# A diffusion-backbone layer on one core: how the feed-forward blocks mark their PSUM banks, begin and end

## The chip, the cores and the metric

The kernel runs on one core of a Trainium2 chip. The metric is the device time of one execution in microseconds (us): the median of repeated runs. Beside it stands one profiled execution, with its own time and its span (first to last instruction). TensorE (PE in the rows) multiplies into PSUM banks, ScalarE (ACT) and VectorE (DVE) work elementwise, GpSimd (POOL) does small work and issues some transfers, SyncE (SP) issues the others.

## The reference

One layer over 512 latent tokens of 1024 channels, with a context prefix of 256 tokens. What matters here is its end: a SwiGLU feed-forward part with 2816 hidden channels, a gated residual, and a last RMSNorm.

```python
def _swiglu(h, w_in, w_out):
    g, u = jnp.split(h @ w_in, 2, axis=-1)
    return (jax.nn.silu(g) * u) @ w_out

        x = x + g1 * mix_lat
        x = x + g2 * _swiglu(_modulate(x, norm_ffn[l], sh2, sc2), w_ffn_in[l], w_ffn_out[l])
    return _rmsnorm(x, norm_final)          # x / sqrt(mean(x^2) + eps) * norm_final
```

All data is 32-bit. The kernel gets the precision by splitting each operand into a high part (a cast to fp32r) and a low part (what the cast lost), and by adding three products: high by high, high by low, low by high.

## The kernel before, in words

Activations lie transposed: 128 channels on the partitions, tokens along the free axis, so x is 8 tiles of 128x512 (`x1[0..7]`). A "half" is 256 of the 512 tokens. `mm3` issues the three products of each pair of 128x128 weight and moving tile, so a sum over n tiles is 3n matmuls (lines 181 to 183). Weights come by SyncE into `wr` or `ur` tiles; ScalarE makes the high part (`wh`, `gh` or `oh`), VectorE the low part (`wl`, `gl` or `ol`).

The hidden channels are 22 tiles. Tiles 0 to 2 are computed plainly, each as two `Half` objects (one for each half of the tokens), which sum a gate and an up product in two banks. Tiles 3 to 21 go through `strassen`, in three runs (3 to 7, 8 to 14, 15 to 21), each followed by the products of its tiles with the second weight (`ffn_out`). The scheme replaces eight half-size products of a tile by seven: with weight quarters A11, A12, A21, A22 and their sums S1 to S4 it issues, 12 matmuls each, A11, S1, S2 and A12 (`front`) and S3, S4 and A22 (`back`, one tile later). The sums are made by `prepare`: VectorE adds, ScalarE casts the high part, VectorE subtracts for the low part; for A12 and A22 ScalarE writes the negated high part and a GpSimd transfer adds the weight to it.

After the A11 product ScalarE copies the bank `x` to a bank `z` (line 1009), and the S2 product is then added on top of `x`, the A12 product on top of the copied `z`. So S2 cannot start before that copy has read `x`. The S1 product is copied to a tile too (line 1013). For a product to be added to what ScalarE or VectorE put in a bank, a matmul must have written those columns before: four plain matmuls do that for the four `pat` banks (line 1180), ahead of the first run of `strassen`. The first run gets tile 3 prepared beforehand (`p3`); the loop then prepares tile j+1 ahead of the products of tile j, and the order written is the order on ScalarE and VectorE as far as a scheduler, which also moves independent instructions, keeps it.

The end: the last seven hidden tiles (15 to 21) multiply the second weight, for each output tile j and half 21 matmuls (`ffn_out`, line 1170 adds the sum to `x1[j]`). Each finished half tile is squared on ScalarE (`SumSq.add`) and summed on VectorE; for the second half the eighth square stays apart and is summed by TensorE with the rest (`urgent`). `rstd_cols` sums over the partitions by matmuls against ones (line 220), GpSimd raises to the power -1/2 (line 224), `rstd_rows` spreads the row over the partitions by two matmuls (line 232). `final` then multiplies each 128x256 piece by `norm_final` and the row, and SyncE writes two pieces at a time (line 1200).

Of the kernel before, what the change touches and what calls it, by code (L numbers as in the profile page):

```python
# [48 lines left out]
def layer_kernel(ctx: ExitStack, tc, xT, cT, w0, w1, wv0, wv, wada_a, wada_b, par, crow, bg, wpool,  # L49
# [140 lines left out]
    class SumSq:  # L190
# [21 lines left out]
        def rstd_cols(self, c):  # L212

            n = (c.stop - c.start) // P
            bank = self.banks.pop(0) if self.banks else PS("pat" if self.free else "ps")
            for i in range(n):
                o = slice(c.start + i * P, c.start + (i + 1) * P)
                terms = [self.q] + [q for s, q in self.last.items() if s == c.start]
                for t, q in enumerate(terms):
                    nc.tensor.matmul(bank[:, 2 * i:2 * i + 2], q[:, o], ones[:, 0:2], start=t == 0, stop=t == len(terms) - 1)  # L220
            sd = tl("rc", [P, 4], F32, 2)
            V.tensor_scalar(sd[:, :n], bank[:, :2 * n].rearrange("p (i w) -> p i w", w=2)[:, :, 0], 1.0 / D, EPS,
                            ALU.mult, ALU.add)
            nc.gpsimd.tensor_tensor(sd[:, :n], sd[:, :n], mhalf[:, :n], ALU.pow)
            return sd
# [812 lines left out]
    def strassen(lo, hi, p=None):  # L1038

        prev = None  # L1040
        p = p or prepared(lo)
        for j in range(lo, hi + 1):
            f = front(j, p) if j < hi else None
            if j + 1 < hi:
                p = prepared(j + 1)
            b = back(j - 1, *prev) if prev else iter(())
            if f:
                next(f)
                next(f)
# [29 lines left out]
    class Half:  # L1079


        def __init__(self, j, c):
            self.c, (self.wg, self.wu, self.dst) = c, pw[j]
            self.accg, self.accu, self.s = PS(), PS(), S("tmp")

        def gate(self):
            mm3(self.accg[:, self.c], self.wg, hpart(self.c))

        def up(self):
            mm3(self.accu[:, self.c], self.wu, hpart(self.c))  # L1090

        def silu(self):
            nc.scalar.activation(self.s[:, self.c], self.accg[:, self.c], AF.Silu)

        def mul(self):
            V.tensor_mul(self.s[:, self.c], self.s[:, self.c], self.accu[:, self.c])
# [68 lines left out]
    def ffn_out(j, c, w, c0, c1):  # L1165

        turn_[0] += 1
        acc = banks[turn_[0] % 3]
        mm3(acc[:, c], w, half(act[c0:c1], c))
# [9 lines left out]
    for i in range(4, 8):  # L1179
        nc.tensor.matmul(banks[i], B11[0][:, :P], B11[0][:, :T], start=True, stop=True)  # L1180
# [10 lines left out]
    def final(i, sd):  # L1191

        c = HALF[i]
        r = st2.rstd_rows(sd, c)
        for j in range(0, KT, 2):
            if j % 4 == 0:
                raw = tl("wr", [P, WMAX], F32, 3)[:, :2 * T].rearrange("p (j t) -> p j t", j=4)
            for e in range(2):
                V.scalar_tensor_tensor(raw[:, j % 4 + e, :], x1[j + e][:, c], pcol(C_NFIN, j + e), r, ALU.mult, ALU.mult)
            nc.sync.dma_start(out.rearrange("p (j t) -> p j t", j=KT)[:, j:j + 2, c], raw[:, j % 4:j % 4 + 2, :])  # L1200

    wl_ = [wchunk(j, c0, c1, (None, None, "wide", "wide", ("oh", "ol"), ("oh", "ol"), None, None)[j], 16) for j in range(KT)]
    for j in range(4):
        ffn_out(j, HALF[0], wl_[j], c0, c1)
# [6 lines left out]
    final(0, sd)  # L1211
    for j in (6, 7):
        ffn_out(j, HALF[1], wl_[j], c0, c1)
    final(1, st2.rstd_cols(HALF[1]))
# [89 lines left out]
```

## Time and profile before

| | before |
|---|---|
| median of 3 runs | 908.22 us (907.78 to 908.56) |
| the profiled execution's own time | 905.2 us |
| its span | 903.4 us |
| mean granted TensorE clock | 0.990 |
| TensorE busy | 879.0 us, 97% |
| VectorE busy | 613.9 us, 68% |
| ScalarE busy | 428.3 us, 47% |

How to read it: the times in the rows run from the span's start. Matmuls overlap, so a row's own duration (0.28 us for 128x256) is longer than the distance to the next start; an idle time stands in brackets at the instruction that ended it, with the engine, tile and line that released it.

### The profile page before, as it was taken

Reading aid. Unit: us, or ns where it says so; the run is one execution under the profiler, and the core shown is the slowest. Engines: PE = TensorE matmul, PEld = TensorE weight load, DVE = VectorE, ACT = ScalarE, POOL = GpSimd, SP = SyncE. Lnnn points to the kernel's source line nnn. Section 1 sums busy time; section 2 is a strip of 40 time slices with the busy share of each in tenths; the row PEclk is TensorE's granted clock in tenths of the full one; section 3 lists DMA queues with packets and bytes.
Section 4 is the critical chain, followed back from the end, with each engine's and each line's share of the span. In section 5 each row is a group of like instructions: output and inputs, shape, how many; then the busy total and the mean of one; then the engine's idle time right before and its main releaser. Section 6 shows DMA issues by size and latency. Waiting matters only on the chain.

```text
span 903.4 us, 14978 instructions
## 1 busy us (share of the span) xinstructions
PE 879.0 (97%) x5883; PEld 796.5 (88%) x5883; DVE 613.9 (68%) x1194; ACT 428.3 (47%) x806; POOL 63.3 (7%) x92
## 2 busy tenths in 40 slices
PE   7999999999999999999999899999999999999996
PEld 6679888899888998889988699999789998899995
DVE  3679656856688676886778768885366754867644
ACT  3455363555343553435553347674145741666520
POOL 0000010010000100001000000111011100111000
PEclk8999999999999999999999999999999999999998
DMA  9834021322066212662147750375356643766402
GB/s 339 323 118 137 22 85 29 133 74 82 24 214 241 83 58 82 210 234 73 57 152 262 247 189 25 100 192 129 94 153 142 158 122 88 203 141 140 118 1 94
DMA packets 42485, 121.20 MB, mean 134 GB/s; under 512 B 4624, under 2 KB 9392, under 8 KB 41392
## 3 DMA queue, kind: packets, MB, share of 16 engines
q1 hardware_dynamic: 36944, 110.29, 37.0%
q0 software_dynamic: 5472, 9.96, 6.5%
q8 instruction: 46, 0.75, 0.3%
q14 instruction: 23, 0.19, 0.1%
HBM read 116.55 MB, written 3.69 MB: 133 GB/s over the span
## 4 chain that ended last, share of the span: by engine, by line
PE 70%; DVE 13%; DMA 9%; issue 4%; ACT 4%; POOL 0%; SPq 0%; POOLq 0%; DVEq 0%; ACTq 0%
PE ps L181 14%; PE ps L183 14%; PE ps L182 14%; DMA pb<-in_wada_b 6%; DVE wl L152 3%; PE pat L326 3%; PE ps L539 2%; PE ps L540 2%; PE ps L538 2%; PE pat L744 2%; PE pat L742 2%; PE pat L743 2%; PE pat L182 2%; PE pat L181 2%; PE pat L183 2%
## 5 line engine op out<-in xcount | busy, mean ns | idle before, releaser
L181 PE MATMUL ps<-a,wh 128*128 128x512 f32 (+1 forms) x368 | 138.8, 377 | 0.0
L182 PE MATMUL ps<-a,wh 128*128 128x512 f32 (+1 forms) x368 | 138.5, 376 | 0.0
L183 PE MATMUL ps<-a,wl 128*128 128x512 f32 (+1 forms) x368 | 138.3, 376 | 0.0
L151 ACT CAST wh<-wr 128x1024 fp32r<-128x1024 f32 (+3 forms) x80 | 80.8, 1012 | 120.2 <-PE ps L182 94.3
L152 DVE TENSOR_TENSOR wl<-wr,wh 128x1024 fp32r<-128x1024 f32 (+3 forms) x80 | 94.3, 1180 | 36.6 <-ACT wh L151 35.4
L183 PE MATMUL ps<-act,wl 128*128 128x512 f32 (+1 forms) x224 | 80.1, 359 | 3.0 <-DVE wl L152 3.0
L181 PE MATMUL ps<-act,wh 128*128 128x512 f32 (+1 forms) x224 | 80.3, 359 | 1.6 <-ACT wh L151 1.0
L182 PE MATMUL ps<-act,wh 128*128 128x512 f32 (+1 forms) x224 | 80.1, 358 | 0.3 <-DVE act L171 0.3
L183 PEld LDWEIGHTS ps<-a,wl 128*128 128x128 f32 x368 | 69.3, 188 | 12.6
L181 PEld LDWEIGHTS ps<-a,wh 128*128 128x128 f32 x368 | 69.3, 188 | 12.2
L182 PEld LDWEIGHTS ps<-a,wh 128*128 128x128 f32 x368 | 69.3, 188 | 11.8
L539 PE MATMUL ps<-wl,a 128*128 128x256 f32 (+1 forms) x192 | 54.6, 284 | 2.2 <-DVE wl L152 2.1
L538 PE MATMUL ps<-wh,a 128*128 128x256 f32 (+1 forms) x192 | 54.1, 282 | 0.5 <-DVE tmp L374 0.5
L540 PE MATMUL ps<-wh,a 128*128 128x256 f32 (+1 forms) x192 | 54.1, 282 | 0.0
L183 PEld LDWEIGHTS ps<-act,wl 128*128 128x128 f32 x224 | 42.5, 190 | 10.3 <-DVE wl L152 4.3
L971 POOL DMA_DIRECT2D ol<-in_wffi x38 | 33.5, 889 | 256.3 <-ACT ol L970 119.4
L181 PE MATMUL ps<-hp,gh 128*128 128x256 f32 x176 | 50.3, 286 | 1.0 <-ACT pat L1009 0.9
L1170 DVE SCALAR_TENSOR_TENSOR x<-ps,lb,x 128x512 f32<-128x512 f32 (+1 forms) x32 | 19.7, 617 | 45.4 <-PE ps L183 45.3
L181 PEld LDWEIGHTS ps<-act,wh 128*128 128x128 f32 x224 | 42.4, 190 | 8.0 <-ACT wh L151 1.5
L182 PE MATMUL ps<-hp,gh 128*128 128x256 f32 x176 | 48.8, 277 | 0.0
L183 PE MATMUL ps<-hp,gl 128*128 128x256 f32 x176 | 48.8, 277 | 0.0
L182 PEld LDWEIGHTS ps<-act,wh 128*128 128x128 f32 x224 | 42.6, 190 | 6.7 <-DVE act L171 0.5
(300 smaller groups left out, 2522.4 us busy)
## 6 DMA issues: line engine op xcount, KB each, us to landing
wr<-in_w SPq DMA_DIRECT2D x42, 512.0 KB, 3.6
pb<-in_wada_b SPq DMA_DIRECT2D x32, 512.0 KB, 4.4
wr<-in_wffi SPq DMA_DIRECT2D x25, 512.0 KB, 4.0
ur<-in_wffi SPq DMA_DIRECT2D x19, 512.0 KB, 4.3
ol<-in_wffi POOLq DMA_DIRECT2D x38, 256.0 KB, 5.1
ada<-in_wada_a SPq DMA_DIRECT2D x8, 1024.0 KB, 7.6
wr<-in_wffo SPq DMA_DIRECT2D x16, 448.0 KB, 3.4
x<-in_xT SPq DMA_DIRECT2D x16, 256.0 KB, 5.7
```

What stands on the lines that cost most here:

```text
L151: nc.scalar.copy(wh, raw[:, :n])
L152: V.tensor_sub(wl, raw[:, :n], wh.bitcast(F32))
L181: nc.tensor.matmul(dst, wh, ah, start=first and i == 0, stop=False, skip_group_check=on)
L182: nc.tensor.matmul(dst, wh, al, start=False, stop=False, skip_group_check=on)
L183: nc.tensor.matmul(dst, wl, ah, start=False, stop=last and i == n - 1, skip_group_check=on)
L326: nc.tensor.matmul(acc0[i], w_first[k][i][w], aT[k][x], start=k + w + x == 0, stop=k == KT - 1 and w == 1)
L538: nc.tensor.matmul(acc[:, :n], ah, wh, start=kk == 0, stop=False)
L539: nc.tensor.matmul(acc[:, :n], ah, wl, start=False, stop=False)
L540: nc.tensor.matmul(acc[:, :n], al, wh, start=False, stop=kk == KT - 1)
L742: nc.tensor.matmul(o, sh_, vh[:, s, :], start=n == 0, stop=False)
L971: nc.gpsimd.dma_start(l, dram, accum_op=ALU.add)
L1170: V.scalar_tensor_tensor(x1[j][:, c], acc[:, c], g2[:, j:j + 1], x1[j][:, c], ALU.mult, ALU.add)
```

## The change

Six edits, in the order of the diff. (1) `rstd_cols` issues all matmuls of the first term, then all of the second; only the first of a bank starts it. (2) When `strassen` is given a prepared tile, the first two steps of `front` (A11 with its copy, S1 with its copy) are written ahead of the preparation of the next tile. (3) The plain tile 2 uses the four `pat` banks, from column 0, and the four marking matmuls of line 1180 are gone. (4) `norm_final` is multiplied by ScalarE into tiles (`ur`, `sg`) as soon as a half tile is finished (`gain`). (5) `final` multiplies several pieces by the row in one VectorE instruction and writes them with one transfer: 4 and 4 pieces in the first half, 4, 3 and 1 in the second. (6) In the last block output tiles 0 and 1 first sum six hidden tiles each, and then the seventh each.

```diff
@@ rstd_cols
-            for i in range(n):
-                o = slice(c.start + i * P, c.start + (i + 1) * P)
-                terms = [self.q] + [q for s, q in self.last.items() if s == c.start]
-                for t, q in enumerate(terms):
-                    nc.tensor.matmul(bank[:, 2 * i:2 * i + 2], q[:, o], ones[:, 0:2], start=t == 0, stop=t == len(terms) - 1)
+            terms = [self.q] + [q for s, q in self.last.items() if s == c.start]
+            for t, q in enumerate(terms):
+                for i in range(n):
+                    o = slice(c.start + i * P, c.start + (i + 1) * P)
+                    nc.tensor.matmul(bank[:, 2 * i:2 * i + 2], q[:, o], ones[:, 0:2], start=t + i == 0,
+                                     stop=t == len(terms) - 1, skip_group_check=True)
@@ strassen
+        early = p is not None
         p = p or prepared(lo)
         for j in range(lo, hi + 1):
             f = front(j, p) if j < hi else None
+            if early:
+                next(f)
+                next(f)
             if j + 1 < hi:
                 p = prepared(j + 1)
             b = back(j - 1, *prev) if prev else iter(())
-            if f:
+            if f and not early:
                 next(f)
                 next(f)
+            early = False
@@ Half
-            self.accg, self.accu, self.s = PS(), PS(), S("tmp")
+            tag = "pat" if j == 2 else "ps"
+            self.accg, self.accu, self.s = PS(tag)[:, :TC], PS(tag)[:, :TC], S("tmp")
@@ ffn_out and what follows
+        if acc is None:
+            acc = ffn_bank()
+            mm3(acc[:, c], w, half(act[c0:c1], c))
         V.scalar_tensor_tensor(x1[j][:, c], acc[:, c], g2[:, j:j + 1], x1[j][:, c], ALU.mult, ALU.add)
         if c1 == FT:
-            for c_ in ((c,) if c != ALL else HALF):
-                st2.add(x1[j][:, c_], c_)
+            st2.add(x1[j][:, c], c)
+            if (j, c) != (KT - 1, HALF[1]):
+                gain(j, HALF.index(c))
-    for i in range(4, 8):
-        nc.tensor.matmul(banks[i], B11[0][:, :P], B11[0][:, :T], start=True, stop=True)
+    def gain(j, i):
+        nc.scalar.activation(gained[i][j][:, 0, :], x1[j][:, HALF[i]], AF.Copy, scale=pcol(C_NFIN, j))
@@ final
-        for j in range(0, KT, 2):
-            if j % 4 == 0:
-                raw = tl("wr", [P, WMAX], F32, 3)[:, :2 * T].rearrange("p (j t) -> p j t", j=4)
-            for e in range(2):
-                V.scalar_tensor_tensor(raw[:, j % 4 + e, :], x1[j + e][:, c], pcol(C_NFIN, j + e), r, ALU.mult, ALU.mult)
-            nc.sync.dma_start(out.rearrange("p (j t) -> p j t", j=KT)[:, j:j + 2, c], raw[:, j % 4:j % 4 + 2, :])
+        for lo, hi in zip(cuts, cuts[1:]):
+            g = ur_[lo // 4][:, lo % 4:(hi - 1) % 4 + 1, :] if i == 0 else sg_[:, lo:hi, :]
+            V.tensor_mul(g, g, r.broadcast_to([P, hi - lo, T // 2]))
+            nc.sync.dma_start(out.rearrange("p (j t) -> p j t", j=KT)[:, lo:hi, c], g)
@@ the last block
+    first = [ffn_bank()[:, :T] for _ in range(2)]
+    for part in (slice(0, FT - c0 - 1), slice(FT - c0 - 1, FT - c0)):
+        for j, acc in enumerate(first):
+            mm3(acc[:, HALF[0]], wl_[j][part], half(act[c0:c1], HALF[0])[part], part.start == 0, part.stop == FT - c0)
```

On ScalarE, where the first run of `strassen` begins (tile 3's last copies, then what follows; `pat_6265` is z and `ps_6260` x of tile 3, the `oh`, `ol` and `gh` tiles from number 6277 on belong to tile 4), before:

```order
L970 ACTIVATE ol_6251<-ur_6169 128x512
L966 CAST oh_6277<-wr_6272 128x512
L966 CAST oh_6287<-wr_6272 128x512
L1097 CAST act_6104<-tmp_6193 128x256
L970 ACTIVATE ol_6288<-wr_6272 128x512
L966 CAST oh_6298<-ur_6273 128x512
L970 ACTIVATE ol_6299<-ur_6273 128x512
L170 CAST gh_6283<-sg_6276 128x1024
L1009 COPY pat_6265<-ps_6260 128x256
L170 CAST wh_6294<-sg_6276 128x1024
L1013 COPY tmp_6328<-ps_6263 128x256
```

The same place of the changed kernel (tile 4's numbers begin at 6300):

```order
L971 ACTIVATE ol_6251<-ur_6169 128x512
L1010 COPY pat_6265<-ps_6260 128x256
L1014 COPY tmp_6293<-ps_6263 128x256
L967 CAST oh_6300<-wr_6295 128x512
L1104 CAST act_6104<-tmp_6193 128x256
L967 CAST oh_6310<-wr_6295 128x512
L971 ACTIVATE ol_6311<-wr_6295 128x512
L967 CAST oh_6321<-ur_6296 128x512
L170 CAST gh_6306<-sg_6299 128x1024
L971 ACTIVATE ol_6322<-ur_6296 128x512
L170 CAST wh_6317<-sg_6299 128x1024
L1021 ACTIVATE tmp_6351<-pat_6265 128x256
```

Both copies of tile 3 moved from behind seven copies of tile 4 to ahead of all of them; they still stand behind tile 3's own A22 copy. On TensorE the order of products at this place was A11, S1 of tile 3, A11 of tile 4, S2, A12 of tile 3; it now is A11, S1, S2, A12 of tile 3, A11 of tile 4, then two matmuls of tile 4's S1, six of tile 3's S3, the other ten of S1, the other six of S3, one of S4, and S2 of tile 4. On VectorE the sum of line 1016 (now 1017, it reads the S2 result) stands ahead of tile 4's `gl` instead of behind its `gl` and `wl`.

On TensorE at the start of the last block, where `act_9120` and `act_9121` are the high and low part of the last hidden tile, `ps_6262` and `ps_6260` the sums of output tiles 0 and 1, and `wh_9172`, `wl_9173` the weights of output tile 1, before:

```order
L183 MATMUL ps_6262<-act_9049,wl_9167 128x256
L181 MATMUL ps_6262<-act_9120,wh_9166 128x256
L181 MATMUL ps_6260<-act_8435,wh_9172 128x256
L182 MATMUL ps_6260<-act_8436,wh_9172 128x256
L182 MATMUL ps_6262<-act_9121,wh_9166 128x256
L183 MATMUL ps_6262<-act_9120,wl_9167 128x256
L183 MATMUL ps_6260<-act_8435,wl_9173 128x256
```

And in the changed kernel (the last hidden tile is `act_9116` and `act_9117`, the weights of output tile 1 are `wh_9171` and `wl_9172`; the line of dots stands for the next 14 products into `ps_6260`):

```order
L183 MATMUL ps_6262<-act_9045,wl_9166 128x256
L181 MATMUL ps_6260<-act_8431,wh_9171 128x256
L182 MATMUL ps_6260<-act_8432,wh_9171 128x256
L183 MATMUL ps_6260<-act_8431,wl_9172 128x256
...
L183 MATMUL ps_6260<-act_9045,wl_9172 128x256
L181 MATMUL ps_6262<-act_9116,wh_9165 128x256
L182 MATMUL ps_6262<-act_9117,wh_9165 128x256
L183 MATMUL ps_6262<-act_9116,wl_9166 128x256
L181 MATMUL ps_6260<-act_9116,wh_9171 128x256
```

The first product with the last hidden tile moved from the 19th place of the block to the 37th; the first that reads the low part of tile 1's weights from the 24th to the 21st.

On VectorE at the end of the second half, from the row's first step on, before:

```order
L222 TENSOR_SCALAR rc_9640<-pat_6266 128x2
L1199 SCALAR_TENSOR_TENSOR wr_9645<-x_928_5289,parm,pat_6267 128x256
L1199 SCALAR_TENSOR_TENSOR wr_9645<-x_929_5291,parm,pat_6267 128x256
L1199 SCALAR_TENSOR_TENSOR wr_9645<-x_930_5293,parm,pat_6267 128x256
L1199 SCALAR_TENSOR_TENSOR wr_9645<-x_931_5295,parm,pat_6267 128x256
L1199 SCALAR_TENSOR_TENSOR wr_9652<-x_932_5297,parm,pat_6267 128x256
L1199 SCALAR_TENSOR_TENSOR wr_9652<-x_933_5299,parm,pat_6267 128x256
L1199 SCALAR_TENSOR_TENSOR wr_9652<-x_934_5301,parm,pat_6267 128x256
L1199 SCALAR_TENSOR_TENSOR wr_9652<-x_935_5303,parm,pat_6267 128x256
```

And in the changed kernel:

```order
L1181 SCALAR_TENSOR_TENSOR x_935_5303<-ps_6262,lb,x_935_5303 128x256
L223 TENSOR_SCALAR rc_9644<-pat_6266 128x2
L1215 TENSOR_TENSOR sg_9162<-sg_9162,pat_6267 128x1024
L1215 TENSOR_TENSOR sg_9162<-sg_9162,pat_6267 128x768
L1215 TENSOR_TENSOR sg_9162<-sg_9162,pat_6267 128x256
```

Eight instructions became three; the first transfer of the second half followed the second instruction and now follows the first, which is four pieces wide. On ScalarE a copy of `gain` stands behind each square of the last block.

## Rows read from the trace of the kernel before

**Rows 1.** The page's first part: busy time, share of the span and instruction count of each engine.

```profile
PE 879.0 (97%) x5883; PEld 796.5 (88%) x5883; DVE 613.9 (68%) x1194; ACT 428.3 (47%) x806; POOL 63.3 (7%) x92
```

**Rows 2.** The timeline of TensorE where the first run of `strassen` begins. Columns: start, duration, engine, line, operation, tiles, shape, count; in brackets the idle time before and its releaser.

```profile
581.05 1.09 PE L1180 MATMUL pat<-hp 128*128 128x512 f32 x4
581.98 0.28 PE L181 MATMUL ps<-hp,oh 128*128 128x256 f32 x1
...
585.07 0.39 PE L181 MATMUL ps<-hp,oh 128*128 128x256 f32 x1
...
586.31 0.39 PE L183 MATMUL ps<-hp,ol 128*128 128x256 f32 x1 [0.73 <-DVE ol L968]
...
588.68 0.39 PE L181 MATMUL ps<-hp,gh 128*128 128x256 f32 x1 [0.94 <-ACT pat L1009]
...
594.24 0.28 PE L181 MATMUL ps<-hp,gh 128*128 128x256 f32 x1
```

**Rows 3.** The timeline of ScalarE at the same place.

```profile
583.88 0.63 ACT L970 ACTIVATE ol<-ur 128x512 fp32r<-128x512 f32 x1
584.41 1.12 ACT L966 CAST oh<-wr 128x512 fp32r<-128x512 f32 x2
...
587.33 1.03 ACT L170 CAST gh<-sg 128x1024 fp32r<-128x1024 f32 x1
588.26 0.36 ACT L1009 COPY pat<-ps 128x256 f32<-128x256 f32 x1
```

**Rows 4.** The timeline of VectorE at the same place.

```profile
587.71 0.69 DVE L990 TENSOR_TENSOR sg<-sg,wr 128x512 f32<-128x512 f32 x1
588.39 1.23 DVE L171 TENSOR_TENSOR gl<-sg,gh 128x1024 fp32r<-128x1024 f32 x1
```

**Rows 5.** The timeline of TensorE at the start of the last block.

```profile
850.68 0.28 PE L181 MATMUL ps<-act,wh 128*128 128x256 f32 x1
...
853.48 0.50 PE L181 MATMUL ps<-act,wh 128*128 128x256 f32 x2 [0.52 <-ACT act L170]
...
854.43 0.39 PE L182 MATMUL ps<-act,wh 128*128 128x256 f32 x1 [0.33 <-DVE act L171]
...
857.00 0.28 PE L181 MATMUL ps<-act,gh 128*128 128x256 f32 x1
```

**Rows 6.** The timeline of VectorE at the same place.

```profile
852.36 0.42 DVE L1034 SCALAR_TENSOR_TENSOR tmp<-ps,tmp 128x256 f32<-128x256 f32 x1
852.69 1.08 DVE L152 TENSOR_TENSOR wl<-wr,wh 128x896 fp32r<-128x896 f32 x1
853.69 0.68 DVE L171 TENSOR_TENSOR act<-tmp,act 128x512 fp32r<-128x512 f32 x1
```

**Rows 7.** The timeline of ScalarE there, and one square from the middle of the last block.

```profile
851.41 0.93 ACT L151 CAST wh<-wr 128x896 fp32r<-128x896 f32 x1
852.81 0.62 ACT L170 CAST act<-tmp 128x512 fp32r<-128x512 f32 x1 [0.47 <-DVE tmp L1034]
...
880.13 0.42 ACT L206 ACTIVATE tmp<-x 128x256 f32<-128x256 f32 x1 [2.06 <-DVE x L1170]
```

**Rows 8.** The timeline of TensorE from the first half's row to the end. An fp32 matmul shows as two.

```profile
884.35 0.51 PE L220 MATMUL pat<-ones,tmp 128*128 128x2 f32 x4
...
887.31 0.60 PE L232 MATMUL pat<-ident,rc 128*128 128x128 f32 x4
...
892.58 0.28 PE L183 MATMUL ps<-act,wl 128*128 128x256 f32 x1
...
893.95 0.83 PE L220 MATMUL pat<-ones,tmp 128*128 128x2 f32 x6 [0.63 <-ACT tmp L206]
895.88 0.86 PE L232 MATMUL pat<-ident,rc 128*128 128x128 f32 x4 [1.10 <-POOL rc L224]
```

**Rows 9.** The timeline of VectorE at the end.

```profile
892.90 0.48 DVE L1170 SCALAR_TENSOR_TENSOR x<-ps,lb,x 128x256 f32<-128x256 f32 x1
894.89 0.16 DVE L222 TENSOR_SCALAR rc<-pat 128x2 f32<-128x2 f32 x1 [1.50 <-PE pat L220]
896.77 3.22 DVE L1199 SCALAR_TENSOR_TENSOR wr<-x,parm,pat 128x256 f32<-128x256 f32 x8 [1.73 <-PE pat L232]
```

**Rows 10.** The first issue of an output transfer of the second half on SyncE's queue.

```profile
897.67 0.37 SPq L1200 DMA_DIRECT2D out<-wr  x1
```

**Rows 11.** Stretches of the span. Columns: the stretch, its length, then busy us (and instructions) of PE, PEld, DVE, ACT, POOL, the granted TensorE clock (1.00 is 2.4 GHz, 0.50 is 1.2 GHz), the busy share of the 16 DMA engines, GB/s.

```profile
898.50:899.50 1.00, 0.00 (x0) 0.00 (x0) 1.00 (x3) 0.00 (x0) 0.00 (x0) 0.50 0.91 298
899.50:900.50 1.00, 0.00 (x0) 0.00 (x0) 0.49 (x2) 0.00 (x0) 0.00 (x0) 0.50 1.03 339
900.50:901.50 1.00, 0.00 (x0) 0.00 (x0) 0.00 (x0) 0.00 (x0) 0.00 (x0) 0.50 1.02 336
901.50:902.50 1.00, 0.00 (x0) 0.00 (x0) 0.00 (x0) 0.00 (x0) 0.00 (x0) 0.50 0.23 76
...
12.30:19.00 6.70, 6.70 (x39) 5.21 (x39) 0.16 (x1) 0.95 (x2) 1.01 (x1) 0.50 1.03 429
505.00:510.50 5.50, 2.37 (x10) 1.34 (x9) 4.63 (x6) 2.70 (x3) 0.00 (x0) 1.00 0.40 131
510.70:513.90 3.20, 3.20 (x9) 2.53 (x8) 0.76 (x2) 1.77 (x3) 0.00 (x0) 0.50 0.81 241
585.00:590.00 5.00, 3.25 (x23) 2.85 (x24) 4.98 (x9) 5.00 (x11) 2.63 (x3) 1.00 0.93 250
```

More of the change, by code (lines that the diff above doesn't have):

```diff
@@ L1163, in layer_kernel, with ffn_bank, ffn_out @@
     turn_ = [0]
-    def ffn_out(j, c, w, c0, c1):
+    def ffn_bank():
         turn_[0] += 1
-        acc = banks[turn_[0] % 3]
-        mm3(acc[:, c], w, half(act[c0:c1], c))
+        return banks[turn_[0] % 3]
+    def ffn_out(j, c, w, c0, c1, acc=None):
+        if acc is None:
+            acc = ffn_bank()
+            mm3(acc[:, c], w, half(act[c0:c1], c))
         V.scalar_tensor_tensor(x1[j][:, c], acc[:, c], g2[:, j:j + 1], x1[j][:, c], ALU.mult, ALU.add)
         if c1 == FT:
-            for c_ in ((c,) if c != ALL else HALF):
-                st2.add(x1[j][:, c_], c_)
+            st2.add(x1[j][:, c], c)
+            if (j, c) != (KT - 1, HALF[1]):
+                gain(j, HALF.index(c))
     def wchunk(j, c0, c1, dst=None, skip=0):
         return wload(wffo[j][:, c0 * P:c1 * P], (c1 - c0) * P, dst, skip)[0]
-    for i in range(4, 8):
-        nc.tensor.matmul(banks[i], B11[0][:, :P], B11[0][:, :T], start=True, stop=True)
     for c0, c1 in ((0, 8), (8, 15)):
@@ L1189, in layer_kernel, with final @@
     SumSq.banks = banks[4:]
[L1191 to L1200 removed]
+    ur_ = [tl("ur", [P, D], F32, 2).rearrange("p (j t) -> p j t", j=4) for _ in range(2)]
+    sg_ = tl("sg", [P, 2 * D], F32, 1, LINE).rearrange("p (j t) -> p j t", j=KT)
+    gained = [[ur_[j // 4][:, j % 4:j % 4 + 1, :] for j in range(KT)], [sg_[:, j:j + 1, :] for j in range(KT)]]
+    def gain(j, i):
+        nc.scalar.activation(gained[i][j][:, 0, :], x1[j][:, HALF[i]], AF.Copy, scale=pcol(C_NFIN, j))
+    def final(i, sd, cuts):
+        c = HALF[i]
+        r = st2.rstd_rows(sd, c).rearrange("p (o t) -> p o t", o=1)
+        for lo, hi in zip(cuts, cuts[1:]):
+            g = ur_[lo // 4][:, lo % 4:(hi - 1) % 4 + 1, :] if i == 0 else sg_[:, lo:hi, :]
+            V.tensor_mul(g, g, r.broadcast_to([P, hi - lo, T // 2]))
+            nc.sync.dma_start(out.rearrange("p (j t) -> p j t", j=KT)[:, lo:hi, c], g)
     wl_ = [wchunk(j, c0, c1, (None, None, "wide", "wide", ("oh", "ol"), ("oh", "ol"), None, None)[j], 16) for j in range(KT)]
+    first = [ffn_bank()[:, :T] for _ in range(2)]
+    for part in (slice(0, FT - c0 - 1), slice(FT - c0 - 1, FT - c0)):
+        for j, acc in enumerate(first):
+            mm3(acc[:, HALF[0]], wl_[j][part], half(act[c0:c1], HALF[0])[part], part.start == 0, part.stop == FT - c0)
     for j in range(4):
[L1204 removed]
+        ffn_out(j, HALF[0], wl_[j], c0, c1, first[j] if j < 2 else None)
     for j in range(4):
@@ L1210, in layer_kernel @@
     ffn_out(5, HALF[1], wl_[5], c0, c1)
-    final(0, sd)
+    final(0, sd, (0, 4, 8))
     for j in (6, 7):
         ffn_out(j, HALF[1], wl_[j], c0, c1)
-    final(1, st2.rstd_cols(HALF[1]))
+    sd = st2.rstd_cols(HALF[1])
+    gain(KT - 1, 1)
+    final(1, sd, (0, 4, 7, 8))
     for n in ("late3", "late2", "late1", "main"):
```

8 lines of the change are left out of this document (4 added, 4 removed).

## The prediction

> **What bounds the kernel now.** The page's first part comes first: TensorE is busy for 879.0 of 903.4 us [rows 1], so an edit pays only where TensorE waits, where it does work that can go, or behind its last product. The whole-span shares say no more; the timelines of the three places that the change touches do. I read TensorE first, then at each idle time the engine that the bracket names.
>
> At the entry of `strassen` [rows 2], TensorE needs 13.19 us from the first marking matmul (581.05) to tile 4's S2 (594.24). From tile 3's S2 (588.68) to there 48 products start in 5.56 us, 0.116 us each. The 84 products of the whole stretch are worth 9.74 us, so 3.45 us are lost: 0.93 in the four marking matmuls (581.05 to 581.98), 0.73 waiting for the low part of tile 4's A11, 0.94 waiting for the copy of x to z, the rest in the wait that ends at 585.07 and in slow starts after waits. Why that copy is late is read on ScalarE [rows 3]: A11 of tile 3 is out by 583.7, the copy starts at 588.26, and ScalarE has no idle time between: it casts tile 4's weights first.
>
> At the start of the last block [rows 5], 42 products (output tiles 0 and 1) take 6.32 us, from 850.68 to 857.00. At the pitch of the entry, 0.116 to 0.118 each, they are worth at most 4.96 us, so some 1.36 us are lost. The brackets name the last hidden tile: its high part comes out of ScalarE at 853.43 [rows 7], its low part out of VectorE at 854.37 [rows 6]. Ahead of that low part VectorE makes the low part of tile 1's weights, done at 853.77 [rows 6]: that is what counts below.
>
> At the end [rows 8 to 10] TensorE's last product is over at 892.86, and 10.5 us follow in one chain: add, square, sum over the partitions, power, spread, multiply, write. The output stream keeps the DMA engines 100% busy at 336 to 339 GB/s from 899.5 on and stops at about 901.7 [rows 11]; VectorE feeds it two pieces at a time until 899.99 [rows 9].
>
> **The change part by part.**
>
> *Entry.* Without marks A11 of tile 3 starts at 581.05, and 24 products later, at 583.83, S2 may start if z is copied. On ScalarE the copy now stands right behind tile 3's last A22 instruction. That one starts at 583.88, and its follower starts at 584.41 [rows 3]; the chain ahead of it (VectorE's sums, ScalarE's casts) doesn't depend on the moved products. So the copy runs from 584.41 to 584.77, and S2 starts 0.06 later as before (588.62 to 588.68), at 584.83: a wait of 1.0 us stays. From there to tile 4's S2 TensorE now has 61 products (S2, A12, A11 of tile 4, S1, S3, one of S4), 7.08 us: 591.91. Two things are late next. Tile 4's copy of x to z stands on ScalarE behind tile 4's casts and three casts of tile 5. Counted from 584.41: two bank copies 0.6, then the casts that took 2.92 before (584.41 to 587.33) less the one that moved behind, 0.54, then 0.93 for `gh` (587.33 to 588.26), 0.5 for that cast, 0.93 for `wh`, 0.3 for a silu, 1.6 for three casts, and the copy 0.36: 592.0, with the hand-over 592.1. That is a second wait of 0.2. The other is `gl`: VectorE's sum for tile 3 now stands ahead of it and costs 0.4, and the sums ahead come 0.15 later, so it ends near 590.2 instead of 589.6 [rows 4]; its first reader is due at 584.83 + 44 x 0.116 = 589.9, so 0.3 is lost there, but the two overlap, since the copy at 592.1 holds TensorE in either case. Gain: 594.24 - 592.1, plus one product that is already done (0.12), less 0.1 for a slow start: **2.1 us**. Bounds: with one or two more casts (0.53 each) ahead of the second copy or in `gl`'s way, 1.2; with no second wait 2.4, and never more than the 3.45 that is lost now. After it everything runs relative to TensorE: what ScalarE and VectorE prepare for tile 5 is behind the same products as before.
>
> *Last block.* 18 products of tile 0 end at 850.68 + 18 x 0.118 = 852.80. Tile 1's high weights are there (851.41 + 0.93 = 852.34 [rows 7]), and its bank, tile 21's x, is read by VectorE until 852.78 [rows 6]. Two products fit, to 853.04; the third reads the low weights, ready at 853.77. VectorE's order here doesn't change, so TensorE waits 0.8 us and goes on at 853.83 with 22 products, which with a slow start end at 856.5. By then the last hidden tile is there (854.37). Gain **0.5 us** against 857.00. Bounds: nothing, if VectorE's subtraction is later by as much; 1.36, the whole loss, if it is early enough.
>
> *End.* (a) Behind the last square stood three matmuls, now two: six rows took 0.83, four rows 0.51 in the first half [rows 8], so about 0.25 less. (b) The first transfer left 0.90 after the row was there (896.77 to 897.67): two multiplies. Now one instruction over 1024 columns stands there. No such instruction with an operand in PSUM is in the rows; the nearest is the subtraction over 1024 columns, 1.23 us [rows 4]; eight instructions over 256 columns with the row in PSUM took 3.22 us [rows 9], 0.40 each. So the stream starts 0.35 later. It is as long as before, since the engines are busy throughout and the runs in DRAM stay 1 KB long: 1.05 MB at 339 are 3.1 us. Fewer instructions on VectorE (2.5 instead of 3.2 us) don't shorten that. The first second ran at 298 GB/s, a little below, so 0.1 comes back: 0.25 later. Sum of (a) and (b): **0.0**. Bounds: 0.5 gain if larger pieces run faster, 0.6 loss if the clock is at its lower level for the whole chain (the spread took 0.86 at the end, partly at 0.50, and 0.60 in the first half [rows 8, 11]).
>
> *At nothing.* Sixteen copies of `gain`, 0.42 each, lie in ScalarE's idle time of 2.06 between two squares [rows 7]; without that cover each would delay a square by 0.42. The first half's multiplications on VectorE shrink, but the last add (892.90) follows TensorE's last product directly already [rows 8, 9]. The other uses of `rstd_cols` have all terms ready, and tile 2's banks are free long before.
>
> **Sum.** 2.1 + 0.5 + 0.0 = 2.6 us off the profiled execution's own 905.2 us: 902.6. The median of the runs shown is 908.22, 3.0 above that execution; the same 0.29% off gives **905.6 us**. About 0.2%, 1.8 us (906.4), is what a measurement of this kernel can tell from no change.
>
> **The rivals.**
>
> *The wait moves* (20%). The copies of tile 3 now stand ahead of tile 4's casts, so tile 4 pays: 0.6 us on ScalarE, which has no idle time from 583.88 to 588.6 and is busy all 5.0 us of 585 to 590, as VectorE is for 4.98 [rows 3, 11]. If a third wait of about 1 us follows, or the last block gains nothing, 1.2 us remain: 907.0, not to be told from no change. Against it: TensorE reaches tile 4's products only two rounds later, with 0.2 to 0.3 short by my count.
>
> *The clock* (6%). After TensorE was busy for only 2.37 of 5.5 us (505 to 510.5) its granted clock was 0.50, 1.2 GHz, for the next 3.2 us; from 12.3 to 19.0 it was 6.7 us [rows 11]. Such a stretch costs half its length, 1.6 or 3.35 us. At the new waits of the entry it would leave 1.0 (907.2) or, at 6.7 us, turn the change into a loss: 908.22 + 0.75 = 909.0. It decides from 5.2 us at half speed on. Against it: in 585 to 590 TensorE now is busy 3.25 of 5 and keeps 1.00 [rows 11], and the change leaves less idle time there. The Trainium skill ("TensorE: Matmul & The Clock Gate", section "HAM oscillation — how this bites in real kernels") says that waits between groups of matmuls can drop the clock again and again; the rows at 510.7 agree, those at 585 show shorter waits without it.
>
> *Larger transfers run faster* (9%). Loads with longer runs reached 429 GB/s in 12.3 to 19.0 [rows 11]. If the output did, 1.05 MB would take 2.44 instead of 3.1 us, the end would come 0.65 earlier, and the time would be 905.0. Against it: the runs stay 1 KB, and the engines are at 100% at 339. The Trainium skill ("DMA: Bandwidth & Descriptors", section "Rules for kernel authors") advises large transfers for the highest bandwidth; no run here shows 512 KB output transfers.
>
> **How the numbers follow.** My forecast (gain 1.9 to 3.2) has 65%, the moved wait 20%, the clock 6% (half of it slower than before), faster transfers 9%. Faster by over 0.2%: 0.65 + 0.09 = 0.74. Within: 0.20 + 0.03 = 0.23. Slower: 0.03. The range leaves out the clock's cases and the tails: the gain from 1.0 (the moved wait with the entry's lower bound) to 4.0 (upper bounds of the last block and the end), 904.2 to 907.2 us.
>
> **What would show it.** Entry: no marking matmuls, one idle time of about 1.0 ending on the copy to z, and tile 4's S2 two us earlier relative to tile 3's first A11. Last block: the idle times on `act` gone, one of 0.8 ending on `wl`. End: four rows instead of six behind the last square, the first output issue about 1.3 us after the spread, the stream again near 339 GB/s. The prediction is wrong if tile 4 or 5 shows new waits of over 0.5 us, if a stretch at 0.50 appears after 580, or if the output stream's length changes.

## The result, and the profile after

The changed kernel took 900.37 us (median of 5 executions, 899.68 to 904.35), before 907.78 (5, 904.12 to 908.56); the ratio is 0.9933, interval 0.991 to 0.9955. Faster, then, but by 7.4 us between the medians (5.9 between the means of the five) instead of 2.6, and outside the range forecast (904.2 to 907.2). The first thing to see is that the two profiled executions don't show 7.4: their spans are 903.4 and 902.6. So the question is not only where the change pays but what else differs between two executions.

The page's first part of the changed kernel, first execution:

```profile
PE 880.6 (98%) x5879; PEld 798.9 (89%) x5879; DVE 612.8 (68%) x1183; ACT 434.0 (48%) x822; POOL 63.2 (7%) x92
```

**Entry**, TensorE's timeline (columns as in [rows 2]), then ScalarE's:

```profile
581.21 0.28 PE L181 MATMUL ps<-hp,oh 128*128 128x256 f32 x1
...
585.08 0.39 PE L181 MATMUL ps<-hp,gh 128*128 128x256 f32 x1 [0.99 <-ACT pat L1010]
...
592.37 0.32 PE L181 MATMUL ps<-hp,gh 128*128 128x256 f32 x1
```

```profile
584.14 0.62 ACT L971 ACTIVATE ol<-ur 128x512 fp32r<-128x512 f32 x1
584.67 0.36 ACT L1010 COPY pat<-ps 128x256 f32<-128x256 f32 x1
...
591.34 0.64 ACT L971 ACTIVATE ol<-wr 128x512 fp32r<-128x512 f32 x1
591.88 0.37 ACT L1010 COPY pat<-ps 128x256 f32<-128x256 f32 x1
```

Against [rows 2, 3]: no marks, one wait of 0.99 on the copy behind the A22 copy, and tile 4's S2 11.16 us after the entry's start instead of 13.19. Tile 4's copy ends at 592.25, and S2 is barely late for it: the second wait of 0.2 shrank to almost nothing.

**Last block** (against [rows 5, 6]): 851.26 to 857.17 are 5.91 us instead of 6.32. The waits on the last hidden tile are gone; the low weights of tile 1 hold TensorE instead.

```profile
851.26 0.28 PE L181 MATMUL ps<-act,wh 128*128 128x256 f32 x1
...
853.64 0.36 PE L181 MATMUL ps<-act,wh 128*128 128x256 f32 x1
853.83 0.28 PE L182 MATMUL ps<-act,wh 128*128 128x256 f32 x1
854.55 0.39 PE L183 MATMUL ps<-act,wl 128*128 128x256 f32 x1 [0.43 <-DVE wl L152]
...
857.17 0.28 PE L181 MATMUL ps<-act,gh 128*128 128x256 f32 x1
```

**End** (against [rows 8 to 11]), TensorE, VectorE, SyncE's queue, and two stretches of the stream:

```profile
892.46 0.28 PE L183 MATMUL ps<-act,wl 128*128 128x256 f32 x1
...
893.83 0.61 PE L220 MATMUL pat<-ones,tmp 128*128 128x2 f32 x4 [0.75 <-ACT tmp L206]
```

```profile
894.55 0.16 DVE L223 TENSOR_SCALAR rc<-pat 128x2 f32<-128x2 f32 x1 [1.28 <-PE pat L220]
896.29 2.42 DVE L1215 TENSOR_TENSOR sg<-sg,pat 128x1024 f32<-128x1024 f32 x3 [1.58 <-PE pat L233]
```

```profile
897.53 1.82 SPq L1216 DMA_DIRECT2D out<-sg  x3
```

```profile
899.00:900.00 1.00, 0.00 (x0) 0.00 (x0) 0.00 (x0) 0.00 (x0) 0.00 (x0) 0.50 1.10 387
900.00:901.00 1.00, 0.00 (x0) 0.00 (x0) 0.00 (x0) 0.00 (x0) 0.00 (x0) 0.50 1.08 383
```

The first issue comes 5.07 us behind the last product (before 5.09). The stream runs at 383 to 387 GB/s instead of 336 to 339. From the last product (its start, here and below) to the end of the span it takes 10.1 us instead of 10.8: the first issue comes 0.02 sooner, the packets take 2.87 us from first to last instead of 3.26, and behind the last landing there are 0.90 us instead of 1.20. Together the three places give 2.0 + 0.4 + 0.7 = 3.1 us; only 0.8 of it shows in the spans, since what lies between differs the other way.

### The profile page after: what moved, and what is told of

The parts are those of the page before. It is cut to its first block, busy times and chain, and to the rows that moved or that the text cites. A ratio compares the mean times of both kernels' runs of the same rounds, so it can differ in the third digit from the quotient of the medians.

```text
span 902.6 us, 14972 instructions
## 1 busy us (share of the span) xinstructions
PE 880.6 (98%) x5879; PEld 798.9 (89%) x5879; DVE 612.8 (68%) x1183; ACT 434.0 (48%) x822; POOL 63.2 (7%) x92
## 4 chain that ended last, share of the span: by engine, by line
PE 69%; DVE 12%; DMA 10%; issue 4%; ACT 3%; SPq 0%; POOL 0%; DVEq 0%; POOLq 0%; ACTq 0%
PE ps L181 14%; PE ps L183 14%; PE ps L182 14%; DMA pb<-in_wada_b 6%; DVE wl L152 3%; PE pat L327 3%; PE ps L540 2%; PE ps L541 2%; PE ps L539 2%; PE pat L745 2%; PE pat L743 2%; PE pat L744 2%; PE pat L182 2%; PE pat L181 2%; PE pat L183 2%
## 5 line engine op out<-in xcount | busy, mean ns | idle before, releaser
L181 PE MATMUL ps<-act,wh 128*128 128x512 f32 (+1 forms) x216 | 78.4, 363 | 1.4 <-ACT wh L151 1.3
L182 PE MATMUL ps<-act,wh 128*128 128x512 f32 (+1 forms) x216 | 78.2, 362 | 0.0
L1181 DVE SCALAR_TENSOR_TENSOR x<-ps,lb,x 128x512 f32<-128x512 f32 (+1 forms) x32 | 19.6, 616 | 45.3 <-PE ps L183 45.3
L181 PEld LDWEIGHTS ps<-act,wh 128*128 128x128 f32 x216 | 41.4, 192 | 8.0 <-ACT wh L151 1.7
L182 PEld LDWEIGHTS ps<-act,wh 128*128 128x128 f32 x216 | 41.3, 191 | 6.5 <-DVE act L171 0.3
```

The costliest lines, as they stand in the source:

```text
L181: nc.tensor.matmul(dst, wh, ah, start=first and i == 0, stop=False, skip_group_check=on)
L182: nc.tensor.matmul(dst, wh, al, start=False, stop=False, skip_group_check=on)
```

## The experiments

All kernels ran, 6 to 12 executions each, beside fresh executions of before (158 in all, in five sets on four chips). Those spread from 898.5 to 912.2 us, with a standard deviation of 2.8 (1.7 to 2.7 within a set); the mean of 12 executions of a kernel is thus uncertain by 0.4 to 0.9, that of six by 1.0. The table gives the difference of the means to the before of the same set, the ratio with its interval (estimated by itself: it is not the quotient of these means), and the mean time at half clock of one execution: 2 x (1 - granted clock) x span, both as each execution reports them. For before that time is 18.2, 18.4, 19.6, 17.4 and 19.7 in the five sets; its standard deviation is 4 us, so a mean of 12 is uncertain by 1.2.

| set | kernel | us against before | ratio (interval) | at half clock, us |
|---|---|---|---|---|
| 1 | all_again | -3.6 | 0.9959 (0.9938 to 0.998) | 15.1 |
| 1 | entry | -2.0 | 0.9983 (0.9961 to 1.0005) | 15.6 |
| 1 | block | +0.4 | 0.9999 (0.9975 to 1.0023) | 18.5 |
| 1 | end | 0.0 | 0.9999 (0.9975 to 1.0022) | 18.0 |
| 2 | noentry | -0.6 | 0.9991 (0.9972 to 1.0009) | 16.4 |
| 2 | always | -1.4 | 0.9987 (0.9963 to 1.001) | 17.4 |
| 2 | early | -1.6 | 0.998 (0.9959 to 1.0001) | 17.5 |
| 2 | cut2 | -2.7 | 0.9957 (0.9938 to 0.9976) | 15.7 |
| 3 | all_third | -1.3 | 0.9981 (0.9962 to 1.0001) | 20.5 |
| 3 | stall | +2.5 | 1.0021 (1.0 to 1.0042) | 23.3 |
| 3 | sgout | 0.0 | 0.9992 (0.9967 to 1.0018) | 19.2 |
| 3 | always2 | -5.3 | 0.9925 (0.99 to 0.9951) | 16.8 |
| 4 | all_fourth | -4.9 | 0.994 (0.9922 to 0.9958) | 15.9 |
| 4 | always2_again | -6.5 | 0.9932 (0.9907 to 0.9958) | 18.0 |
| 5 | before_again | +0.5 | 1.0006 (0.9985 to 1.0028) | 19.8 |
| 5 | entry_again | -4.7 | 0.9955 (0.9933 to 0.9978) | 16.2 |
| 5 | noentry_again | -1.8 | 0.9978 (0.9953 to 1.0004) | 17.3 |
| 5 | all_fifth | -6.6 | 0.9928 (0.9904 to 0.9951) | 14.6 |

**The whole change again** (no edit): all_again, all_third, all_fourth, all_fifth.

> The whole change once more. In its first profile the three places together gain 3.1 us (entry 2.0, last block 0.4, end 0.7), but its median lay 7.4 us below. Theory A (spread): the rest is the spread between executions, above all the pace of the 128x256 products, which in both traces is 0.113 us in some stretches and 0.118 in others, and the length of the stretch at half clock near 508; then this run's median lies 2 to 5 us below before. Theory B (the pace belongs to the change): 6 to 8 us below again, with more of the products at 0.113 than in the first profile.

> The whole change a third time, beside new executions of before. Theory A (the change is worth its 3.1 us of the traces plus up to 1 us of clock, and the first comparison's 7.4 was five executions against five of a kernel whose executions spread by 2.5 us): mean 2.5 to 4.5 us below before. Theory B (the change is worth 6 us or more on some chips): 6 to 8 us below.

> The whole change beside a fourth set of executions of before. Theory A (3.1 us of the traces plus up to 1 us of clock, hidden in a spread of 2.3 us between executions): mean 2 to 4.5 us below before, and the pooled difference of the last three calls near 3. Theory B (7.4 us, as first measured, on some chips): 6 to 8 us below.

> The whole change on the same chip as the three others: the sum of the entry alone and the rest alone, 3 to 4 us (theory A), or 5 us where before takes 907 or more (theories B and C).

The gain is 3.6, 1.3, 4.9 and 6.6 us, 4.1 in the mean: more than chance alone, with intervals that don't all meet. Before has means of 903.8, 905.8, 907.7 and 907.6 in these sets, the changed kernel 900.3, 904.5, 902.8 and 901.0. So neither theory holds alone: the traces' 3.1 is in the middle, and the first comparison (5.9 by the means) is no freak either.

**The entry alone, and the change without it.** `entry` is the diff's hunks of `strassen`, `Half` and line 1180; `early` the first of these alone; `noentry` all but these three. Of the edits here and below only the lines that matter are printed.

```diff
@@ early
             f = front(j, p) if j < hi else None
+            if early:
+                next(f)
+                next(f)
             if j + 1 < hi:
                 p = prepared(j + 1)
...
```

> Only edits 2 and 3 (early copies, marks on tile 2's banks). My sum: 2.1 us below before (the changed kernel's trace shows 2.0 at this place). Rival (the copies start a faster stretch of products): over 4 us below. Rival (the moved wait takes it back): less than 1 us.

> Only edit 2 (early copies; the four marking matmuls of 0.93 us stay). If ScalarE sets S2 of tile 3 (copy behind the A22 copies), the marks lie in the shadow of that wait: the wait at S2 falls from 1.0 to 0.1, tile 4's S2 comes at the same time after the last plain product as with both edits, and the gain is about 2 us as with both. If the marks' 0.93 us stand on the path, the gain is 1.1 us.

> The whole change without edits 2 and 3 (the entry as before). Theory A (the entry gives its 2.0 us of waits, and also 1.4 us because its waits before sometimes drop the clock: the entry alone had 15.6 us at half clock per execution, before 18.2): mean about 1.0 to 1.3 us below before (last block 0.5, end 0.7), half-clock time near 18 us again. Theory B (the clock is chance): half-clock time near 15.5 us as in the whole change, mean 2.5 us below before.

> Edits 2 and 3 alone, once more. On the chip of the fourth comparison before took 907.7 us in the mean and the whole change 902.8 (899.0 and 894.9 with the half-clock time taken off), on the two others 903.8 to 905.8 and 900.3 to 904.5. Theory A (the entry carries the whole of the clock's part and 2 us of waits): 2 to 3 us below before on any chip. Theory B (what differs between chips sits in the entry): 4 us below where before takes 907 or more.

> Edits 1, 4, 5 and 6 without the entry. Theory A: 0.6 to 1.3 us below before on any chip. Theory B: the same; theory C (what differs between chips sits in the last block or the end): 3 us below where before takes 907 or more.

The times: `entry` gains 2.0 and 4.7 us, the change without it 0.6 and 1.8. Means over both sets are 3.4 and 1.2, uncertain by 0.5 each: 4.6 together, against 4.1 for the whole change. In the first set the parts (2.0, -0.4 for `block`, 0.0 for `end`) don't add up to its 3.6; the gap of 2.0 is uncertain by 1.4.

Place by place the traces agree far better than the times. From the entry's start to tile 4's S2, read as above, eight traces of kernels with edits 2 and 3 (`cut2` is one) give 11.0 to 11.2 us. `early` gives 11.57: with the marks still there it has all but 0.4 to 0.6 of the gain, since half of their 0.93 lies in the shadow of the wait for the copy. At tile 5's S2 it has all of it: 21.1 us after the entry's start against 20.5 to 21.8 in the eight traces (mean 21.2). So no run shows that what the missing marks gain lasts beyond tile 5. Seven traces with the old entry fall in two groups: 13.2 to 13.5 (`before`, `before_again`, `end`, `noentry`, `noentry_again`), and 14.9 and 15.0 (`block`, `sgout`). The stretches of `block` (columns as in [rows 11]), and under them the same waits in `before`, show why:

```profile
580.00:585.00 5.00, 3.21 (x23) 2.60 (x22) 5.00 (x9) 5.00 (x11) 2.62 (x3) 1.00 0.99 277
585.00:588.40 3.40, 3.40 (x17) 3.40 (x17) 2.65 (x4) 1.80 (x4) 0.00 (x0) 0.50 1.08 270
588.40:592.00 3.60, 3.60 (x33) 3.60 (x32) 2.85 (x5) 2.54 (x5) 0.87 (x1) 1.00 0.76 216
```

```profile
583.87:588.87 5.00, 3.22 (x23) 2.61 (x22) 5.00 (x9) 5.00 (x11) 2.63 (x3) 1.00 0.92 266
```

In `block`, after 3.21 busy us of 5, the clock is 0.50, 1.2 GHz, for 3.4 us, in which 17 products fit instead of some 30. In `before` the same waits, 3.22 busy us of 5, left it at 1.00. The old entry drops the clock in some executions and not in others; the new one did so in none of 12 traces. The times at half clock don't settle how much that is worth: `noentry` and `noentry_again`, with the old entry, spend 2.0 and 2.4 us less there than before, as much as the whole change saves in the mean.

One wait is new. In five of the eight traces with edits 2 and 3 (`entry`, `entry_again`, `cut2`, `all_third`, `all_fifth`) tile 5's S2 waits 0.40 to 0.97 us for its copy; in no trace with the old entry does it wait over 0.1. `all_fifth`, TensorE, VectorE, ScalarE:

```profile
599.77 0.38 PE L181 MATMUL ps<-hp,gh 128*128 128x256 f32 x1 [0.97 <-ACT pat L1010]
```

```profile
595.78 0.69 DVE L984 TENSOR_TENSOR sg<-ur 128x512 f32<-128x512 f32 x1 [1.21 <-DMA ur<-in_wffi]
```

```profile
596.84 0.62 ACT L170 CAST act<-tmp 128x512 fp32r<-128x512 f32 x1 [1.57 <-DVE tmp L1035]
...
599.36 0.36 ACT L1010 COPY pat<-ps 128x256 f32<-128x256 f32 x1
```

Tile 6's weights are late: VectorE waits for their transfer, ScalarE's cast behind it for VectorE (line 1035), and tile 5's copy stands behind that cast. With edits 2 and 3 the transfer is issued 7.9 to 8.0 us after the entry's start and takes 7.2 to 9.7 us to land; with the old entry it is issued at 6.8 to 6.9 and takes 4.9 to 7.5. Over the whole first run of `strassen`, from the entry's start to the first product of `ffn_out`, seven traces with the old entry take 51.6 to 54.6 us (mean 53.2), the eight with edits 2 and 3 take 49.9 to 51.4 (mean 50.6): 2.6 us in all.

**Longer waits at the entry.**

```diff
@@ front
-        nc.scalar.copy(z, x)
+        for _ in range(6 if j == NP else 1):
+            nc.scalar.copy(z, x)
```

> Before, with five more copies of the same bank on ScalarE ahead of tile 3's S2, so that TensorE waits 2 to 3 us longer at the entry. Theory A (waits of TensorE here drop the granted clock in some executions): more time at half clock than before's 18.3 us, by 1.7 to 6.8 us, a stretch at 0.50 between 585 and 600 in the trace, and a mean 3 to 6 us above before. Theory B (the clock does not follow these waits): half-clock time as before, mean above before by the added wait alone.

The trace has a stretch at 0.50 from 587.9 to 591.3, and the time at half clock is 23.3 us against 19.6, as theory A has it. With `block` and `sgout` it is the third of eight traces with waits of the old kind. The time doesn't decide: the wait grew by 1.5 us (2.47 instead of 0.95), and the mean of 2.5 above before, uncertain by 1.0, is less than theory A's 3 to 6 and not clear of the wait alone.

**Last block alone** (the hunk of the last block, with `ffn_bank`):

> Only edit 6 (first two output tiles of the last block side by side). My sum: 0.4 to 0.5 us below before, within what can be told. Rival (a faster pace behind the new wait, 0.113 instead of 0.118 for the block's products up to 863): 0.3 more.

The effect is too small for its time to tell; its trace does: 5.81 us from the block's start to output tile 2, against 6.32. Over all traces the old order takes 6.1 to 6.7, the new one 5.4 to 6.3, 0.55 less in the mean.

**The end alone, its pieces and its source.** `end` is the hunks of `rstd_cols`, `gain` and `final`.

```diff
@@ cut2
-    final(0, sd, (0, 4, 8))
+    final(0, sd, (0, 2, 4, 6, 8))
-    final(1, sd, (0, 4, 7, 8))
+    final(1, sd, (0, 2, 4, 6, 8))
...
@@ sgout (on before)
+            if j == 0 and i == 1:
+                sg_ = tl("sg", [P, 2 * D], F32, 1, LINE)
-                raw = tl("wr", [P, WMAX], F32, 3)[:, :2 * T].rearrange("p (j t) -> p j t", j=4)
+                raw = (tl("wr", [P, WMAX], F32, 3)[:, :2 * T] if i == 0 else sg_[:, j * TC:j * TC + 2 * T]).rearrange("p (j t) -> p j t", j=4)
```

> Only edits 1, 4 and 5 (rstd order, gain on ScalarE, wide multiply and transfers). My sum on record: 0.0. Rival (larger transfers run faster; the changed kernel's trace shows 387 GB/s and 0.7 us less behind the last product): 0.7 us below before.

> The whole change with the output in pieces of two tiles (256 KB transfers as before) behind multiplications over 512 columns. If the size of the transfers made the stream faster (387 GB/s instead of 336), it is near 336 again, and the time from the last product to the end is 10.3 to 10.5 us (start 0.6 earlier, stream 0.4 longer than 10.1). If the faster stream came from VectorE, which reads and writes less, it stays at 387 and the end is at 9.6 to 9.8.

> Before, with one change: the second half's output pieces are written to the sg tile, from which the changed kernel sends them, by the same eight three-operand instructions and the same four transfers of 256 KB. If the place of the source decides, the packets of 1 KB take 46 ns each as in the changed kernel and the stream runs at 383 to 387 GB/s; the end is 0.3 to 0.4 us earlier behind the last product than before's 10.7 to 10.8. If VectorE's instructions decide, it stays at 324 to 350 GB/s with packets of 49 ns.

The time of `end` shows no gain (0.0, uncertain by 0.8); its trace does. From the last product to the end: 10.7 to 10.8 us with the old end (11.1 to 11.2 in the three traces where the clock fell soonest behind the last product), 10.1 with the new (10.6 in one such trace). Transfers of half the size run just as fast, `cut2`:

```profile
897.80:898.80 1.00, 0.00 (x0) 0.00 (x0) 0.42 (x1) 0.00 (x0) 0.00 (x0) 0.50 1.09 382
898.80:899.80 1.00, 0.00 (x0) 0.00 (x0) 0.00 (x0) 0.00 (x0) 0.00 (x0) 0.50 1.09 386
```

and so does the old end's stream, once its source is `sg`, wherever VectorE's eight instructions don't hold it up (`sgout`, VectorE done at 901.05):

```profile
900.90:901.40 0.50, 0.00 (x0) 0.00 (x0) 0.15 (x1) 0.00 (x0) 0.00 (x0) 0.50 0.88 307
901.40:901.90 0.50, 0.00 (x0) 0.00 (x0) 0.00 (x0) 0.00 (x0) 0.00 (x0) 0.50 1.08 383
```

A 1 KB packet takes 46 ns from `sg` in every trace, with either end, and 49 on average from `wr`; the first half's output, sent from `ur` in transfers of 512 KB, takes 48 to 49. So the tile that the output is sent from decides the packets' rate (one trace, `sgout`, with the old end), not the size of the transfers; why `wr` is slower was not tried. But `sgout` gains nothing (10.8), for the issues come no sooner. SyncE's queue in `before` and in `sgout`:

```profile
897.67 2.72 SPq L1200 DMA_DIRECT2D out<-wr  x4
```

```profile
898.73 2.72 SPq L1202 DMA_DIRECT2D out<-sg  x4
```

Two multiplications take 0.78 us for 256 KB, 335 GB/s: VectorE fed the old stream at the very rate that it had. It takes the faster source and the wide multiplication (2.42 us) together; the wide one with `wr` as source was not run. And 0.3 of the 0.7 us has nothing to do with the rate. In all nine traces in which three transfers end the program 0.9 us follow the last landing, in all eleven with four 1.2: SyncE steps through its waits on transfers at 0.06 us each, six of which are left by then in `before` and one in the changed kernel. So `cut2`, whose stream is as fast, ends 10.3 us after the last product and not 9.6 to 9.8, also because its first issue came only 0.17 sooner.

**Copies early for every tile.**

```diff
@@ always: strassen, on the changed kernel
-            if early:
+            if f:
                 next(f)
                 next(f)
+            if rest:
+                next(rest)
+                rest = None
```

Here `rest` is what is left of tile 3's preparation, its A22 copies; `always2` has the pieces of `cut2` too.

> The whole change, with the two copies of A11 and S1 written ahead of the next tile's preparation for every tile, and tile 3's A22 copies behind them. My theory: the 1.0 us wait of S2 in tile 3 falls to 0.1, and the short wait of S2 in the later tiles (0.12 each in the fast pace, behind which the pace can change from 0.113 to 0.118) goes; 1 to 3 us below the whole change. Rival (ScalarE only shifts the wait to gh or wh of the next tile): same as the whole change.

> Copies ahead of the next tile's preparation for every tile, as before with that edit, and output pieces of two tiles. If the earlier copies and the earlier first output pay as the traces of the two apart suggest (waits of the entry 0.3 us shorter, no short waits at S2 of the later tiles, first output 0.6 us earlier), the mean is 4 to 5 us below before and below the whole change's; if the pace of the products hides it, it cannot be told from the whole change.

> The version with early copies for every tile and output pieces of two tiles, once more (six executions so far, 5.3 us below before and 4.0 below the whole change of the same call). If its gain is its own: 1 to 2 us below the whole change. If those six were chance: the same as the whole change within 1 us.

The wait at tile 3's S2 is gone, and tile 4's S2 comes no sooner (11.2 to 11.3 us): waits on `gh` and `gl` of 0.18 and 0.76 (in `always2_again` 0.76 alone) took its place, the rival. Tile 5's S2 waits in none of the three traces; tile 6's weights are asked for 6.8 to 6.9 us after the entry's start again. `always` was 1.3 above `cut2` beside it, `always2` 4.0 and 1.6 below the whole change in six executions each; these differences are uncertain by 1.0 to 1.3. The traces give `always2` 0.24 at the end (9.9 us) and all three together 0.8 in the first run of `strassen` (49.8 us in the mean), part of it pace; the rest of its lead they don't explain, and it stays open whether it is real.

**A second trace of before:**

> The kernel before, unchanged, so that a second trace of it stands beside the first, and a null comparison. Expected by every theory: no difference from the other executions of before. If executions differ by the pace of the products and by the stretches at half clock alone, its trace shows the same waits as the first one to 0.1 us at the entry and at the end, and differs in these two.

Its waits at the entry are those of the first (13.27 us), and yet it is 3.8 us longer. From the entry to the last block it takes 4.05 us more, with the clock at 1.00 in both: that is the pace. At the end it takes 0.4 more, since the clock fell sooner there.

## Why the prediction was wrong, point by point

**The base.** The step that failed first was the one from the sum to the forecast: 905.2 - 2.6, scaled to a median of three, 908.22, with a range of 3 us. Before has a mean of 905.8 over 158 executions, and single ones 7 us to either side. Of the 5.2 us between the forecast 905.6 and 900.37, 2.4 are this base (908.2 for 905.8), 1.5 the gain (4.1 in the mean of four sets, for 2.6), and the remaining 1.3 lie within the spread of five executions: I take them for chance. That 0.2% is about what can be told holds within one set (the intervals are 0.18 to 0.26% to either side), but not for an absolute time from another chip or hour. What spreads them stands in the rows of one trace. TensorE fully busy with the same products, in the changed kernel's first execution (columns as in [rows 11]; products in brackets):

```profile
594.00:604.00 10.00, 10.00 (x91) 10.00 (x90) 9.60 (x16) 7.35 (x13) 1.75 (x2) 1.00 0.99 234
614.00:624.00 10.00, 10.00 (x87) 10.00 (x87) 4.05 (x7) 4.10 (x8) 0.87 (x1) 1.00 0.57 148
```

From start to start the one is a pace of 0.1133 us, the other of 0.1178, both at granted clock 1.00. The pace changes behind a wait, be it a short one, here at S2 of a tile:

```profile
611.00 0.28 PE L181 MATMUL ps<-hp,wh 128*128 128x256 f32 x1
611.11 0.28 PE L182 MATMUL ps<-hp,wh 128*128 128x256 f32 x1
611.23 0.28 PE L183 MATMUL ps<-hp,wl 128*128 128x256 f32 x1
611.35 0.38 PE L181 MATMUL ps<-hp,gh 128*128 128x256 f32 x1
611.57 0.28 PE L182 MATMUL ps<-hp,gh 128*128 128x256 f32 x1
...
611.81 0.28 PE L181 MATMUL ps<-hp,gh 128*128 128x256 f32 x1
611.93 0.28 PE L182 MATMUL ps<-hp,gh 128*128 128x256 f32 x1
612.04 0.28 PE L183 MATMUL ps<-hp,gl 128*128 128x256 f32 x1
```

Steps of 0.11 to 0.12 us before (0.113 on average), one of 0.22 at S2, and of some 0.12 behind. Wherever the pace changes in the three runs, in any of the 20 traces, there is such a step of 0.15 us or more; not every one changes it. I had read "0.116 to 0.118" as one figure with noise. The three runs of `strassen` have some 410, 580 and 580 products, so each can differ by 1.9 to 2.6 us from one execution to the next: in `before_again` some 1200 of them came at the slower pace, in `before` some 100. `always`, which has no waits at S2 of the later tiles, kept one pace through each run, and the slower one through all of the last.

**Entry.** Predicted 2.1; the first pair of traces gives 2.03, and all traces without a drop 2.0 to 2.5. The mechanism was right up to tile 4's S2 in every step but the second wait. The step that failed is the one behind it, "what ScalarE and VectorE prepare for tile 5 is behind the same products as before": products came 2 us sooner and a transfer of weights 1.2 us later. So the rival "the wait moves" came in part, at tile 5: nothing in the first profile, 0.40 to 0.97 us in five of eight traces, four of them over the 0.5 that I had named as a sign of being wrong.

**The clock.** This rival was looked at from the wrong side. "It now keeps 1.00" was read from a single execution; in other executions the old waits do drop it, at 1.6 us each. Taking the waits away can therefore be worth more than their length. By the table, kernels with the whole change spend 14.6, 15.1, 15.9 and 20.5 us at half clock against 17.4 to 19.7: in the mean some 2 us less, worth 1 us. But without the entry it is 2 us less too, so that this saving sits in the entry is not shown. The Trainium skill ("TensorE: Matmul & The Clock Gate", section "HAM oscillation — how this bites in real kernels") says that waits between groups of matmuls can drop the clock repeatedly; `block`, `sgout` and `stall` agree, at 585 to 591; `before` and four others with the same waits show none there.

**The pace behind the entry.** It was in no term. In the first run of `strassen` the kernels with the old entry had 295 of some 410 products at the slower pace (mean of 8 traces), those with the early copies 158 (12 traces): 137 x 0.0045 = 0.6 us. With so few traces this may be chance.

**Last block.** Predicted 0.5, measured 0.41 in the first pair, 0.55 over all; the wait for the low weights came as forecast, though of 0.43 and not 0.8, with a slower stretch ahead of it.

**End.** Predicted 0.0, measured 0.6 to 0.7. (a) was right: 2.09 us from the last product to the row's first step instead of 2.31. Of (b), the late start was right, 1.24 us from the row to the first issue where I had 1.25, but "as long as before" failed: I took 336 to 339 GB/s for the limit of transfers with runs of 1 KB. It was what one source tile gave and what VectorE fed, both at once, so "fewer instructions on VectorE don't shorten that" was wrong too. That is 0.4 of the 0.7; the other 0.3, the stretch behind the last landing, stood in no term. The rival "larger transfers" had the right sign for the wrong reason: fewer transfers gave the 0.3, not faster ones. The advice of the Trainium skill cited with it ("DMA: Bandwidth & Descriptors", section "Rules for kernel authors") made no difference to the rate here: 256 KB ran like 512 KB.

**Sum.** At the entry 2.2 of waits, 0.5 of clock (1.6 us in two of seven traces), 0.6 of pace, less 0.4 for the new wait at tile 5, are 2.9 by count and 2.6 by the whole first run. With 0.55 and 0.6 the sum is 3.8 us, against 4.1 in the mean and 1.3 to 6.6 in the sets. In set 5 the parts add up (4.7 + 1.8 = 6.5 against 6.6), and both are larger there than in the other sets; with an uncertainty of 0.7 to 0.9 in each that shows no place. Why before is slower on two of the four chips and the changed kernel is not, stays open.

## What to carry to other kernels

Read several executions before taking a median as a base: the spread between them is itself in the trace, as the number of products in stretches of equal length and the granted clock. A wait that leaves the clock alone in one trace can drop it in the next, so that waits on TensorE cost their length and sometimes a half-speed stretch behind them. When a wait goes, look in several traces at what is prepared two tiles on: a transfer that was in time may not be any more. Before calling a transfer rate a limit, work out at what rate the transfers are issued, and look for the same transfer from another tile.

## What the hardware showed that I had not expected

Two paces of the same fp32r product over 256 columns, 0.1133 and 0.1178 us at the same granted clock, changed only behind a wait, and often kept for hundreds of products; packets of 1 KB of 46 ns from one SBUF tile and 49 ns, single ones up to 82, from another; 0.06 us for each finished transfer that SyncE still has to step through at the end of the program.
